# A hybrid decoder step on one core: norm broadcasts one block later, two rooms exchanged, residual stores in GpSimd's queue, idle products behind the last sums

## The chip, the cores and the metric

The kernel runs on one core of one Trainium2 chip. A core has a matrix engine (TensorE, PE in the rows; PEld is its weight load), VectorE (DVE), ScalarE (ACT), GpSimd (POOL) and SyncE (SP), which run their own instruction streams in order and wait for one another by semaphores, and 16 DMA engines that move data between memory and the core. The metric is the time of one execution on the device in microseconds (us), and lower is better.

## The reference

One inference step of a one-layer decoder: 1024 prompt tokens behind 16 meta tokens, and 32 tokens of running sequences. Attention heads with a window and Mamba-2 heads run side by side on a projection of the normalized input. Their outputs are normalized, joined and projected back, then a squared-ReLU MLP follows, and a last norm:

```python
def mix_and_mlp(h, ao, so, attn_out_g, w_out, norm2_g, w_up, w_down):
    mix = jnp.concatenate([rmsnorm(ao, attn_out_g), so], axis=-1)
    h = h + mix @ w_out
    u = jax.nn.relu(rmsnorm(h, norm2_g) @ w_up)
    return h + (u * u) @ w_down
...
    y_prompt = rmsnorm(hp, norm_f_g)[:, N_META:]
    y_sample = rmsnorm(hs, norm_f_g)
```

The width is 1024 and the MLP's inner width 4096. All is in float32. After w_in, only 1056 tokens (32 and 1024) are carried, with the features on the 128 partitions: a tile of the hidden state is 8 feature blocks by 1056 tokens.

## The kernel before

**Matrix products.** An operand is split into a high part of fewer bits and a low remainder (ScalarE casts the high part, VectorE or GpSimd subtracts it), and a product is three matmuls: high by high, high by low, low by high. The MLP's two matrices are multiplied by a seven-product scheme of 2 by 2 blocks (products 1 to 7, by token half and feature half).

**Order.** The code is written in the order in which steps are meant to run; a scheduler then places the instructions of each engine, and each engine's order is fixed. A tile of a ring with few buffers makes its next writer wait for the last reader. So the order on an engine says who is held up behind a wait.

**The stretch with the output projection (some 418 to 472 us).** `wout_stream` runs the second half of w_out in two passes. In the first pass, eight feature blocks m by two token chunks (288 and 384 tokens), a block's step is: PE multiplies, VectorE adds the product into the residual `ha` (L918), ScalarE squares it into `s2` (L923, one buffer), GpSimd adds that square to the running sum `sq` (L924), and the residual is stored to `he` in memory (L967, L970), from where it is read back at 805 us and later. `gained` (L928) then scales block m - 1 in place by norm2's gain, so it must wait until the store of that block has landed. The loop at L1414 runs the second pass, one chunk of 384 tokens by eight blocks; its store (L1419) is issued by GpSimd. Weights come through rings: `load_wout` loads a raw block on SyncE's queue (L231, two buffers), ScalarE casts it (L234), and GpSimd or VectorE subtracts (L235); even blocks are called `whi`, odd ones `wlo`.

**Norm 2.** `row_norm` is a generator for each of three token chunks. Its first step sums `sq` over the partitions on PE (a product with a column of ones, `c<-ones,sq`) and takes the power -0.5 on GpSimd (L311), the second makes diagonal matrices on VectorE (`dg`, L1181), the third spreads them over the partitions on PE (`c<-dg,ones`) and copies the result to `rb` (L1193). The loop at L1414 calls a step of these behind each block. `rb` is used by the MLP's squared ReLU (L1283).

**Early pairs.** The first six column blocks p of w_up begin with products 1 and 2 alone (`pre` in `run_up`). Product 1 is copied out by ScalarE (`copies`, L1268), product 2 goes through the squared ReLU into a tile called `b11`, which GpSimd stores (L1300). `b11` lives in one of two rooms, `s2` and `s3`, of one buffer each. In the main steps that follow, the copies of product 6 take room `s2` and those of product 7 room `s3`.

**The end.** `final_last` treats the last quarter of tokens: after the last product of w_down, VectorE adds, ScalarE squares (L1690), PE sums over the partitions (`c<-ones,q`), VectorE and GpSimd take the power, VectorE makes three diagonals (L1588), PE spreads them, VectorE multiplies (L1599), and four stores of y end the kernel. Six products of ones by ones into a bank that nobody reads (`idle2`) are there to keep PE busy.

Of the kernel before, what the change touches and what calls it, by code (L numbers as in the profile page):

```python
# [9 lines left out]
F32 = mybir.dt.float32  # L10
# [25 lines left out]
TH, TQ = TM // 2, TM // 4  # L36
# [155 lines left out]
def body(ctx: ExitStack, tc: tile.TileContext, xT, xm, win, wdt, wo, wu, wd, ck, cv, sc, st, sT, vec, consts,  # L192
# [45 lines left out]
    class Ahead:  # L238
# [9 lines left out]
        def next(self):  # L248
            while self.fns and len(self.got) <= self.n:
                self.more()  # L250
            return self.got.pop(0)
# [680 lines left out]
    def wout_stream():  # L932

        ws = {}
        for m, ch in [(0, 0), (0, 1), (1, 0), (1, 1), (0, 2), (1, 2)] + [(m, ch) for m in range(2, 8) for ch in range(3)]:
            c0, cw = CM[ch]
            if m not in ws:
                ws[m] = weights.next()
            hb = sp.tile([128, 384], F32, name="hb", tag="hb", bufs=3)[:, :cw]
            SP.dma_start(out=hb, in_=xm[:, 8 * c0 + m * cw:8 * c0 + (m + 1) * cw])  # L940
            ps = gps()
            gemm(ps[:, :cw], ws[m], X[ch])
            DVE.tensor_tensor(out=hb, in0=hb, in1=ps[:, :cw], op=ALU.add)
            SP.dma_start(out=hd[:, m, c0:c0 + cw], in_=hb)
            yield
        acta_s.close()
        opb = act_s.enter_context(pool("opb", side="right"))

        ha = xn["ha"] = opb.tile([128, 8, TM], F32, name="ha")
        c2 = CM[2][0]  # L950
        first = [load_kept(0, ch, sp) for ch in range(2)]
        SP.dma_start(out=ha[:, 1], in_=hd[:, 1])
        SP.dma_start(out=ha[:, 2], in_=hd[:, 2])
        SP.dma_start(out=ha[:, 0, c2:], in_=hd[:, 0, c2:])
        for m in range(3, 8):
            SP.dma_start(out=ha[:, m], in_=hd[:, m])
        sq01 = opb.tile([128, CM[2][0]], F32, name="sq01")
        sq.update({ch: sq01[:, CM[ch][0]:CM[ch + 1][0]] for ch in range(2)})
        pieces = [(m, ch) for m in range(8) for ch in range(2)]
        for m, ch in pieces:  # L960
            c0, cw = CM[ch]
            if ch == 0:
                w = weights.next()
            hb = ha[:, m, c0:c0 + cw] if m else first[ch]
            mixer_half(m, ch, w, hb, sp, POOL)
            if m == 0:
                SP.dma_start(out=he[:, m, c0:c0 + cw], in_=hb)  # L967
                gained(m, ha[:, m, c0:c0 + cw], hb)
            elif ch == 1:
                SP.dma_start(out=he[:, m, 0:c2], in_=ha[:, m, 0:c2])  # L970
                if m > 1:
                    gained(m - 1, ha[:, m - 1, 0:c2], ha[:, m - 1, 0:c2])
            yield
        gained(7, ha[:, 7, 0:c2], ha[:, 7, 0:c2])
# [314 lines left out]
    def run_up(p, j):  # L1289
        pre = p < NPRE  # L1290
        if pre and j == 1:
            chain[p, "a"] = [bank("b" if p % 2 else "g") for _ in range(2)]
            product(chain[p, "a"], p, 1, True)
            s_[p, 1] = copies("s1", chain[p, "a"], 2)
            POOL.dma_start(out=s1d[p], in_=s_[p, 1])
        elif pre and j == 2:
            product(chain[p, "a"], p, 2, False)
            b = pu.tile([128, 2, TQ], F32, name="b11", tag="s2" if p % 2 else "s3", bufs=1)
            relu2_of(b, chain[p, "a"])
            POOL.dma_start(out=u7[p][:, 4], in_=b.rearrange("p c t -> p (c t)"))  # L1300
        elif j == 5:
            us[p] = pu.tile([128, 4, TH], F32, name="u", tag="u", bufs=2)
            if pre:
                s_[p, 1] = pu.tile([128, 2, TQ], F32, name="s1", tag="s1", bufs=2)
                SP.dma_start(out=s_[p, 1], in_=s1d[p])
                chain[p, "a"] = [bank("g") for _ in range(2)]
                for c in range(2):
                    ACT.copy(out=chain[p, "a"][c][:, :TQ], in_=s_[p, 1][:, c])
                SP.dma_start(out=us[p][:, 0], in_=u7[p][:, 4])
            chain[p, "b"] = [bank("b") for _ in range(2)]  # L1310
            product(chain[p, "b"], p, 5, True)
        elif j == 1:
            chain[p, "a"] = [bank("g") for _ in range(2)]
            product(chain[p, "a"], p, 1, True)
            s_[p, 1] = copies("s1", chain[p, "a"], 2)
        elif j == 2:
            cc = [bank("c") for _ in range(2)]
            product(cc, p, 2, True)
            sums(quad(p, 0), cc, s_[p, 1])
            relu2(us[p][:, 0], 0)  # L1320
        elif j in (6, 7):
            product(chain[p, "a"], p, j, False)
            s_[p, j] = copies("s2" if j == 6 else "s3", chain[p, "a"])
            if j == 7:
                sums(quad(p, 2), chain[p, "b"], s_[p, 7])
                relu2(us[p][:, 2], 1)
        elif j == 4:
            product(chain[p, "a"], p, 4, False)
            relu2_of(quad(p, 1), chain[p, "a"])
        else:  # L1330
            product(chain[p, "b"], p, 3, False)
            sums(quad(p, 3), chain[p, "b"], s_[p, 6])
            relu2(us[p][:, 3], 1)
            u, t = us[p], pu.tile([128, 4, TH], F32, name="t", tag="x", bufs=2)
            tt = DVE.tensor_tensor
            tt(out=t[:, 0], in0=u[:, 3], in1=u[:, 0], op=ALU.subtract)
            tt(out=t[:, 2], in0=u[:, 2], in1=u[:, 3], op=ALU.subtract)
            tt(out=t[:, 1], in0=u[:, 2], in1=t[:, 0], op=ALU.subtract)
            tt(out=t[:, 3], in0=u[:, 1], in1=t[:, 1], op=ALU.subtract)
            a = 1 if pre else 0  # L1340
            POOL.dma_start(out=u7[p][:, 4 + a:7], in_=u[:, a:3])  # L1341
            POOL.dma_start(out=u7[p][:, 0:4], in_=t)
# [71 lines left out]
    for m in range(8):  # L1414
        w = ahead
        if m < 7:
            ahead = weights.next()
        mixer_half(m, 2, w, bs[:, m, c2:], nw, DVE)
        POOL.dma_start(out=he[:, m, c2:], in_=bs[:, m, c2:])  # L1419
        gained(m, xn["b22" if m > 3 else "b12"][:, m % 4, c2 - TH:], bs[:, m, c2:])  # L1420
        if m < 6:
            next(norms2[m // 3], None)
        if m in (0, 2):
            operand(xa, "b21" if m else "b11")
            split_op("b21" if m else "b11", bs[:, 2 * m:2 * m + 4, 0:TH])
        elif m == 3:
            for n, name in enumerate(("b12", "b22")):
                ACT.copy(out=xn[name][:, :, 0:CM[2][0] - TH], in_=bs[:, 4 * n:4 * n + 4, TH:c2])
            prepare(1)
        elif m == 4:  # L1430
            DVE.tensor_tensor(out=xn["b11"], in0=xn["b12"], in1=bs[:, 0:4, 0:TH], op=ALU.subtract)
            prepare(2)
        elif m == 5:
            ACT.copy(out=xn["b21"], in_=bs[:, 4:8, 0:TH])
# [238 lines left out]
    def final_last():  # L1673

        hc = h[:, :, two(1)]
        q2 = hpool.tile([128, 4, TQ], F32, name="q2", tag="q2", bufs=2)
        ACT.activation(out=q2[:, 0:3], in_=hc[:, 0:3], func=AF.Square)
        for n in (0, 1, 2):
            DVE.tensor_tensor(out=sums2[1], in0=sums2[1], in1=q2[:, n], op=ALU.add)
        yield  # L1680
        for m in range(3):
            gained(1, m)
        yield
        pt = sum_tokens("c", sums2[1])
        yield
        yield
        part = hpool.tile([128, 3], F32, name="rp3")
        DVE.tensor_scalar(out=part, in0=pt[:, 0:3], scalar1=1.0 / D, scalar2=EPS, op0=ALU.mult, op1=ALU.add)
        yield
        ACT.activation(out=q2[:, 3], in_=hc[:, 3], func=AF.Square)  # L1690
        pt = sum_tokens("c", q2[:, 3])

        for _ in range(6):
            mm(idle2[:, 0:128], ones, ones, True, True)
        rs = hpool.tile([128, 3], F32, name="rs3", tag="rs3", bufs=2)
        DVE.scalar_tensor_tensor(out=rs, in0=pt[:, 0:3], scalar=1.0 / D, in1=part, op0=ALU.mult, op1=ALU.add)
        POOL.tensor_tensor(out=rs, in0=rs, in1=nhalf[:, 0:3], op=ALU.pow)
        gained(1, 3)
        ps = spread("c", [diag(rs, q) for q in range(3)])
        for m, n, q in ((4, 2, SP), (6, 2, ACT), (0, 3, SP), (3, 1, ACT)):  # L1700
            normed(1, ps, m, n)
            q.dma_start(out=y[:, 1, m:m + n], in_=hc[:, m:m + n])
# [62 lines left out]
```

## Time and profile before

| what | value |
|---|---|
| time, median of 3 runs | 1152.06 us (1151.73 to 1154.35) |
| the profiled execution's own time | 1152.0 us |
| its span (first to last instruction) | 1150.2 us |
| mean granted PE clock | 0.992 |
| busy: PE, PEld, DVE, ACT, POOL | 97%, 94%, 74%, 49%, 21% |
| memory traffic | read 125.49 MB, written 50.72 MB |

A row of the timeline has the start in us from the span's start, the length in us, engine, source line, operation, output<-input, and in brackets the idle time before it and who ended it. A row of the waits has the waiting engine and line, who was waited for, the total in us, the number and the longest. A row of the windows has, for a stretch, its length and then each engine's busy us with its number of instructions (PE, PEld, DVE, ACT, POOL), the granted PE clock (1.00 is full speed), the DMA engines' busy share and GB/s. In the rows for one source line, three numbers are ns at least, median and at most; "DMA to landing" is from a transfer's issue to its arrival.

### The profile page before, as it was taken

Reading aid. Unit: us, or ns where it says so; the run is one execution under the profiler, and the core shown is the slowest. Engines: PE = TensorE matmul, PEld = TensorE weight load, DVE = VectorE, ACT = ScalarE, POOL = GpSimd, SP = SyncE. Lnnn points to the kernel's source line nnn. Section 1 sums busy time; section 2 is a strip of 40 time slices with the busy share of each in tenths; the row PEclk is TensorE's granted clock in tenths of the full one; section 3 lists DMA queues with packets and bytes.
Section 4 is the critical chain, followed back from the end, with each engine's and each line's share of the span. In section 5 each row is a group of like instructions: output and inputs, shape, how many; then the busy total and the mean of one; then the engine's idle time right before and its main releaser. Section 6 shows DMA issues by size and latency. Waiting matters only on the chain.

```text
span 1150.2 us, 21730 instructions
## 1 busy us (share of the span) xinstructions
PE 1115.8 (97%) x8399; PEld 1076.4 (94%) x8399; DVE 850.5 (74%) x1654; ACT 566.5 (49%) x1192; POOL 239.5 (21%) x258
## 2 busy tenths in 40 slices
PE   7999999999999999999999999999999999999997
PEld 6999988898888899999999999999999999999997
DVE  7566788997489975997777677766589656768483
ACT  7312465756476647854444444444434344546461
POOL 4533343534345456210000000000000000000000
PEclk9899999999999999999999999999999999999998
DMA  8301101011286466665645243343999654465273
GB/s 292 116 30 45 37 21 36 19 47 58 61 252 202 149 222 230 214 206 178 216 154 183 104 158 151 133 157 123 359 312 323 207 176 114 117 189 166 84 236 100
DMA packets 84424, 177.64 MB, mean 154 GB/s; under 512 B 10692, under 2 KB 32740, under 8 KB 82272
## 3 DMA queue, kind: packets, MB, share of 16 engines
q1 hardware_dynamic: 77392, 141.58, 39.2%
q0 software_dynamic: 6224, 33.74, 7.4%
q8 instruction: 66, 1.08, 0.4%
q10 hardware_dynamic: 704, 0.93, 0.2%
q14 instruction: 38, 0.31, 0.1%
HBM read 125.49 MB, written 50.72 MB: 153 GB/s over the span
## 4 chain that ended last, share of the span: by engine, by line
PE 71%; DVE 14%; issue 5%; DMA 5%; ACT 4%; POOL 1%; POOLq 0%; SPq 0%; DVEq 0%; ACTq 0%
PE g L202 40%; PE b L202 17%; PE c L202 9%; PE s L202 2%; PE o L202 1%; DVE bc L512 1%; DVE p L638 1%; DVE xs L512 1%; ACT p L640 1%; DVE Qs L671 1%; DMA cb<-in_xT 1%; DMA wdr<-in_wd 1%; DVE Sd L1534 1%; DVE cb L437 1%; PE y L202 1%
## 5 line engine op out<-in xcount | busy, mean ns | idle before, releaser
L202 PE MATMUL g<-acth,whi 128*128 128x384 f32 (+2 forms) x624 | 194.8, 333 | 0.2 <-ACT acth L396 0.2
L202 PE MATMUL g<-acth,wlo 128*128 128x384 f32 (+2 forms) x624 | 192.3, 329 | 1.7 <-POOL wlo L225 0.8
L202 PE MATMUL g<-actl,whi 128*128 128x384 f32 (+2 forms) x528 | 174.5, 330 | 2.6 <-DVE actl L397 2.6
L202 PEld LDWEIGHTS g<-acth,wlo 128*128 128x128 f32 x624 | 116.2, 190 | 4.5 <-issue 1.6
L202 PEld LDWEIGHTS g<-acth,whi 128*128 128x128 f32 x624 | 116.1, 190 | 3.0 <-issue 2.0
L1547 ACT CAST ts<-tr 128x528 fp32r<-128x528 f32 x92 | 58.2, 632 | 115.5 <-PE b L202 98.0
L202 PEld LDWEIGHTS g<-actl,whi 128*128 128x128 f32 x528 | 100.5, 190 | 5.4 <-DVE actl L397 4.2
L1548 DVE TENSOR_TENSOR ts<-tr,ts 128x528 fp32r<-128x528 f32 x92 | 65.1, 708 | 53.9 <-ACT ts L1547 50.3
L311 POOL TENSOR_TENSOR rs<-rs,nhalf 128x3 f32<-128x3 f32 x9 | 9.0, 996 | 312.8 <-DVE rs L310 312.7
L1268 ACT COPY s<-g 128x264 f32<-128x264 f32 x90 | 33.9, 379 | 71.3 <-PE g L202 64.4
L1273 DVE TENSOR_TENSOR u<-b,s 128x264 f32<-128x264 f32 x64 | 27.4, 431 | 25.2 <-PE b L202 14.3
L225 POOL TENSOR_TENSOR wlo<-wraw,whi 128x1024 fp32r<-128x1024 f32 (+1 forms) x18 | 41.5, 2309 | 17.8 <-ACT whi L224 17.6
L1341 POOL DMA_DIRECT2D u<-u x16 | 8.5, 532 | 175.6 <-ACT u L1284 142.4
L1278 ACT ACTIVATE u<-u 128x528 f32<-128x528 f32 x42 | 27.1, 646 | 27.5 <-DVE u L1277 27.5
L202 PE MATMUL b<-ts,w7y 128*128 128x264 f32 x279 | 39.3, 285 | 0.0
L202 PE MATMUL g<-ts,whi 128*128 128x264 f32 x279 | 38.9, 284 | 0.0
L202 PE MATMUL g<-ts,w7y 128*128 128x264 f32 x279 | 38.9, 283 | 0.0
L202 PE MATMUL b<-ts,whi 128*128 128x264 f32 x279 | 38.9, 284 | 0.0
L202 PE MATMUL g<-ts,wlo 128*128 128x264 f32 x270 | 38.0, 285 | 0.0
L202 PE MATMUL b<-ts,wlo 128*128 128x264 f32 x270 | 37.3, 282 | 0.0
L640 ACT ACTIVATE p<-p,nm 128x256 f32<-128x256 f32 (+1 forms) x64 | 31.3, 491 | 11.5 <-DVE nm L638 11.4
L202 PEld LDWEIGHTS b<-ts,w7y 128*128 128x128 f32 x279 | 36.1, 188 | 0.0
(557 smaller groups left out, 3365.9 us busy)
## 6 DMA issues: line engine op xcount, KB each, us to landing
tr<-u SPq DMA_DIRECT2D x92, 264.0 KB, 3.3
wraw<-in_wu SPq DMA_DIRECT2D x38, 512.0 KB, 4.0
wdr<-in_wd SPq DMA_DIRECT2D x68, 256.0 KB, 3.7
u<-t POOLq DMA_DIRECT2D x16, 1056.0 KB, 5.5
wraw<-in_win SPq DMA_DIRECT2D x16, 512.0 KB, 3.7
u<-u POOLq DMA_DIRECT2D x10, 792.0 KB, 3.6
wraw<-in_wo SPq DMA_DIRECT2D x24, 256.0 KB, 3.0
h<-he SPq DMA_DIRECT2D x16, 264.0 KB, 4.9
```

The lines of the kernel that those rows point to most:

```text
L202: PE.matmul(out, lhsT=a, rhs=b, start=start, stop=stop, skip_group_check=on)
L225: eng.tensor_tensor(out=lo[:, k], in0=raw[:, k], in1=f(hi[:, k]), op=ALU.subtract)
L437: DVE.tensor_tensor(out=out, in0=ps, in1=rb1[:, c0:c0 + cw], op=ALU.mult)
L512: DVE.scalar_tensor_tensor(out=acc, in0=cb[:, j:j + CL], scalar=cw_(j), in1=acc, op0=ALU.mult, op1=ALU.add)
L638: DVE.tensor_tensor_reduce(out=s_out, in0=ps, in1=mask, scale=-scale, scalar=nsink, op0=ALU.add, op1=ALU.min, accum_out=nm)
L640: ACT.activation(out=s_out, in_=s_out, func=AF.Exp, bias=nm, scale=-1.0, accum_out=sm)
L671: DVE.tensor_tensor(out=Q[oth, g, :, :rows], in0=src, in1=f(Q[own, g, :, :rows]), op=ALU.subtract)
L1268: ACT.copy(out=s[:, c], in_=ps[c][:, :TQ])
L1273: DVE.tensor_tensor(out=out[:, c], in0=ps[c][:, :TQ], in1=s[:, c], op=ALU.add)
L1278: ACT.activation(out=x, in_=x, func=AF.Square)
L1547: ACT.copy(out=t[:, 0], in_=x)
L1548: DVE.tensor_tensor(out=t[:, 1], in0=x, in1=f(t[:, 0]), op=ALU.subtract)
```

## The change

Four edits. The stores of the residual in the first pass are issued by GpSimd instead of SyncE. The two rooms of `b11` are exchanged: even p take `s2`, odd p `s3`. In the loop of the second pass, the steps of norm 2's first chunk are called behind blocks 0, 1 and 3 (0, 1 and 2 before) and those of the second chunk behind blocks 3, 4 and 6 (3, 4 and 5 before). The six idle products at the end take `q2`, the tile that ScalarE squares last, as stationary operand, so that they can't start before it is written, and stand behind the sums over it.

```diff
@@ wout_stream
             if m == 0:
-                SP.dma_start(out=he[:, m, c0:c0 + cw], in_=hb)
+                POOL.dma_start(out=he[:, m, c0:c0 + cw], in_=hb)
                 gained(m, ha[:, m, c0:c0 + cw], hb)
             elif ch == 1:
-                SP.dma_start(out=he[:, m, 0:c2], in_=ha[:, m, 0:c2])
+                POOL.dma_start(out=he[:, m, 0:c2], in_=ha[:, m, 0:c2])
                 if m > 1:
                     gained(m - 1, ha[:, m - 1, 0:c2], ha[:, m - 1, 0:c2])
@@ run_up
-            b = pu.tile([128, 2, TQ], F32, name="b11", tag="s2" if p % 2 else "s3", bufs=1)
+            b = pu.tile([128, 2, TQ], F32, name="b11", tag="s3" if p % 2 else "s2", bufs=1)
@@ the loop of the second pass
-        if m < 6:
-            next(norms2[m // 3], None)
+        for n in range(2):
+
+            if m - 3 * n in (0, 1, 3):
+                next(norms2[n], None)
@@ final_last
         for _ in range(6):
-            mm(idle2[:, 0:128], ones, ones, True, True)
+            mm(idle2[:, 0:128], q2[:, 3, 0:128], ones, True, True)
```

Each engine's order changes with it. On SyncE the nine stores are gone from between the loads of w_out. On ScalarE, in the first pass (`s_4784` to `s_4889` are the squares of block 1, chunk 1 to block 4, chunk 0; `ha<-ha,vec` is `gained`, `wlo` and `whi` are the casts of the weights of blocks 5 and 6, `xb11h` is a cast for the MLP):

```order
 L923 ACTIVATE s_4784<-ha 128x384
 L923 ACTIVATE s_4807<-ha 128x288
+L928 ACTIVATE ha<-ha,vec 128x672
 L923 ACTIVATE s_4824<-ha 128x384
+L1166 CAST xb11h<-ha 128x1056
 L923 ACTIVATE s_4848<-ha 128x288
+L928 ACTIVATE ha<-ha,vec 128x672
+L234 CAST wlo<-wraw 128x512
 L923 ACTIVATE s_4865<-ha 128x384
-L928 ACTIVATE ha<-ha,vec 128x672
+L234 CAST whi<-wraw 128x512
 L923 ACTIVATE s_4889<-ha 128x288
```

The scaling of block m, which waits for the landing of that block's store, now stands between the two squares of block m + 1, and the casts of the weights come two squares earlier.

On PE, in the second pass, around the spread of the second chunk (`dg_5209`; `whi` is block 6, `wlo` block 7):

```order
 L202 MATMUL g<-acth_3131,whi 128x384 x2
 L202 MATMUL g<-actl_3133,whi 128x384
+L202 MATMUL g<-acth_3131,whi 128x384 x2
+L202 MATMUL g<-actl_3133,whi 128x384
 L202 MATMUL g<-acth_3131,whi 128x384
 L202 MATMUL c<-dg_5209,ones 128x128 x3
-L202 MATMUL g<-acth_3131,whi 128x384
-L202 MATMUL g<-actl_3133,whi 128x384
-L202 MATMUL g<-acth_3131,whi 128x384
 L202 MATMUL g<-acth_3131,wlo 128x384
 L202 MATMUL g<-actl_3133,wlo 128x384
```

The spread stands three matmuls later, behind the whole of block 6.

On PE at the end (`q_13375` is the last squared tile, `dg_13449` to `dg_13453` are the three diagonals):

```order
 L202 MATMUL b<-tk_12732,w_15_13028 128x264 x3
-L202 MATMUL g<-ones 128x128 x5
 L202 MATMUL c<-ones,q_13375 128x1 x3
-L202 MATMUL g<-ones 128x128
+L202 MATMUL g<-ones,q_13375 128x128 x6
 L202 MATMUL c<-dg_13449,ones 128x128
 L202 MATMUL c<-dg_13451,ones 128x128
 L202 MATMUL c<-dg_13453,ones 128x128
```

Five of the six idle products stood ahead of the sums, one behind; now all six stand behind.

## The prediction

> **What bounds the kernel now.** I read the busy times first, then who PE waits for, then those places on the timeline. The page's first part:
>
> ```profile
> PE 1115.8 (97%) x8399; PEld 1076.4 (94%) x8399; DVE 850.5 (74%) x1654; ACT 566.5 (49%) x1192; POOL 239.5 (21%) x258
> ```
>
> PE sets the time: a change that adds no product can only win what PE waits. PE's waits between 400 and 520 us:
>
> ```profile
> PE c L202 <- DVE dg L1181: 2.1, 2, 1.6
> PE g L202 <- ACT s L1268: 2.1, 1, 2.1
> ...
> PE g L202 <- POOL wlo L235: 0.5, 1, 0.5
> PE g L202 <- ACT wlo L234: 0.4, 1, 0.4
> ```
>
> All of them lie where the first three edits act. The fourth acts on the end, behind the last product, where everything is one chain. PE at these places, on the timeline:
>
> ```profile
> 440.28 0.54 PE L202 MATMUL g<-acth,wlo 128*128 128x288 f32 x2 [0.48 <-POOL wlo L235]
> ...
> 468.86 0.91 PE L202 MATMUL c<-dg,ones 128*128 128x128 f32 x6 [1.60 <-DVE dg L1181]
> ...
> 481.52 0.91 PE L202 MATMUL c<-dg,ones 128*128 128x128 f32 x6 [0.53 <-DVE dg L1181]
> ...
> 517.69 0.39 PE L202 MATMUL g<-xt3h,w7x 128*128 128x264 f32 x1 [2.12 <-ACT s L1268]
> ```
>
> The sum below is made against the profiled execution's own 1152.0 us (span 1150.2), which is the median of the runs shown (1152.06) to 0.1 us.
>
> **The stores in GpSimd's queue, and the broadcasts.** These two share one stretch, from 438 to 482 us, and one sum. SyncE, ScalarE, GpSimd and VectorE there:
>
> ```profile
> 428.09 4.00 SPq L970 DMA_DIRECT2D he<-ha  x2
> 432.18 0.53 SPq L231 DMA_DIRECT2D wraw<-in_wo  x1
> ...
> 437.52 0.84 ACT L928 ACTIVATE ha<-ha,vec 128x672 f32<-128x672 f32 x1
> 438.26 0.60 ACT L234 CAST wlo<-wraw 128x512 fp32r<-128x512 f32 x1
> ...
> 463.69 0.62 ACT L234 CAST whi<-wraw 128x512 fp32r<-128x512 f32 x1 [0.74 <-DMA wraw<-in_wo]
> ```
> ```profile
> 428.19 0.80 POOL L924 TENSOR_TENSOR sq<-sq,s 128x288 f32<-128x288 f32 x1
> 429.63 1.01 POOL L924 TENSOR_TENSOR sq<-sq,s 128x384 f32<-128x384 f32 x1 [0.64 <-ACT s L923]
> 438.94 1.28 POOL L235 TENSOR_TENSOR wlo<-wraw,wlo 128x512 fp32r<-128x512 f32 x1 [0.45 <-ACT wlo L234]
> ```
> ```profile
> 464.34 0.69 DVE L235 TENSOR_TENSOR whi<-wraw,whi 128x512 fp32r<-128x512 f32 x1 [0.89 <-ACT whi L234]
> ...
> 468.16 0.56 DVE L1181 TENSOR_TENSOR dg<-cs,rs 128x384 f32<-128x384 f32 x1
> ...
> 478.06 0.55 DVE L924 TENSOR_TENSOR sq<-sq,s 128x384 f32<-128x384 f32 x1
> ```
>
> Removed: nine stores from SyncE's queue. The load of block 5's weights at 432.18 stood behind the stores of blocks 1 and 2, which wait for the residual (SyncE is held from 428.09 to 432.09). Without them it can go at some 425 us. With the cast placed earlier on ScalarE, PE's 0.41 + 0.48 us before 440.28 are to be had.
>
> Added on GpSimd: nine issues of about 0.54 us (the rows of its own stores, below), 4.9 us. They cost nothing while they lie beside a square on ScalarE: behind each 288-wide addition GpSimd already waits for the next square (0.64 us at 429.63), and the store waits for the same VectorE addition that the square waits for.
>
> What the move does cost is the landing. `gained` of block m waits for its store and now stands in ScalarE's queue ahead of the second square of block m + 1. Behind it are queued that square, GpSimd's addition, the casts, the splits and PE. Landing times, of SyncE's stores in this stretch and of those that GpSimd issues today:
>
> ```profile
> L970 SPq DMA_DIRECT2D he<-ha x7: 319/320/340, 428.1 to 452.5; - x7
> ...
> DMA to landing us min/median/max: 2.2/3.1/7.5
> ```
> ```profile
> L1419 POOL DMA_DIRECT2D he<-ha x8: 539/539/628, 455.6 to 473.4; - x8
> ...
> DMA to landing us min/median/max: 2.8/4.1/5.7
> ```
>
> Block 1's store can be issued when GpSimd has made the addition of 428.19, at 429.0. That moment is crowded by the loads of `ha`; I take 4.7 us, between GpSimd's median and its maximum, so 433.7. ScalarE then has a scaling (0.84), a square (0.5), a cast of 1.1, a square behind GpSimd's addition (0.5), a scaling and the cast of block 5: 437.9. GpSimd issues block 3's store and splits (1.28): 439.7 instead of 440.22. So of 0.9 us some 0.4 are won; with 3.9 us of landing nearly all, and with 7.5 us 2.4 are lost. In the Trainium skill, "DMA: Bandwidth & Descriptors", section "Specifications", GpSimd's path has a first byte after about 1 us and SyncE's after 0.6; the medians differ by 1.0 here, so the rows decide; by the page alone this term would be 0.6 us better.
>
> The spread at 468.86 waited for a VectorE that was late:
>
> ```profile
> 465.00:470.00 5.00, 3.40 (x22) 3.10 (x22) 5.00 (x9) 4.32 (x9) 0.72 (x2) 1.00 0.72 210
> 470.00:475.00 5.00, 5.00 (x37) 4.96 (x36) 4.97 (x9) 5.00 (x9) 1.60 (x3) 1.00 0.61 208
> ```
>
> The third busy time is VectorE's: full from 464.34 on. It began late since the weights of block 6 had just landed (the 0.74 at ScalarE, the 0.89 at VectorE). Three matmuls more ahead of the spread (0.17 us each by the steps of PE's rows) would cover 0.5 of the 1.60 alone; the rest must come from VectorE being earlier. Now the load of block 6 stands behind one w_up load, not two, and the cast that frees its room stands four ScalarE instructions earlier. I put VectorE 1 us earlier at the diagonals; it could be none, if ScalarE lags behind the stores, or 2. But the chain does not end at the spread: the third chunk's sums need the addition of 478.06, behind the same full VectorE, and a PE that comes 2.5 us early waits there. The 0.53 before 481.52 follows from those sums and stays. So the stretch wins what VectorE wins: 1.0 us, between a loss of 0.5 and a gain of 2.5 (0.9 + 1.6).
>
> **The rooms.** The copies of product 6 of the first main pair stand behind the store of the last early pair:
>
> ```profile
> 517.25 0.66 ACT L1268 COPY s<-g 128x264 f32<-128x264 f32 x2 [3.46 <-DMA u<-b]
> ```
> ```profile
> 506.64 0.54 POOL L1300 DMA_DIRECT2D u<-b  x1 [3.78 <-ACT b L1284]
> ...
> 511.77 0.54 POOL L1300 DMA_DIRECT2D u<-b  x1 [3.71 <-ACT b L1284]
> ```
>
> The store of pair 5 goes at 511.77 and lands at 517.2. After the exchange product 6 needs the store of pair 4, five us earlier, and PE goes on at 515.6. Next late is product 7's copy, which now needs pair 5's store. It is wanted at about 517.0, and PE needs it one product (2.9 us) after 515.6, at 518.4. A weight cast that stood at 517.80 is ahead of it, so it may end at 518.6. That is 0.0 to 0.4 lost of 2.12; I take 1.9 won. Weights and operands behind are split 5 us or more before use.
>
> **The idle products.** The end, on PE, and VectorE's first multiplication:
>
> ```profile
> 1138.36 1.28 PE L202 MATMUL g<-ones 128*128 128x128 f32 x10
> 1139.50 0.83 PE L202 MATMUL c<-ones,q 128*128 128x1 f32 x6
> 1140.19 0.47 PE L202 MATMUL g<-ones 128*128 128x128 f32 x2
> 1141.98 1.56 PE L202 MATMUL c<-dg,ones 128*128 128x128 f32 x6 [1.33 <-DVE dg L1588]
> ```
> ```profile
> 457.83 0.94 PE L202 MATMUL c<-dg,ones 128*128 128x128 f32 x6
> ```
> ```profile
> 172.60:172.70 0.10, 0.00 (x0) 0.00 (x0) 0.10 (x1) 0.10 (x1) 0.00 (x0) 0.82 0.31 82
> 176.00:176.10 0.10, 0.10 (x2) 0.10 (x2) 0.10 (x1) 0.00 (x0) 0.00 (x0) 0.61 0.00 0
> 1142.00:1142.10 0.10, 0.10 (x1) 0.10 (x2) 0.10 (x2) 0.00 (x0) 0.00 (x0) 0.75 0.00 0
> ```
> ```profile
> 513.99:517.40 3.41, 1.58 (x14) 1.37 (x12) 1.71 (x3) 0.15 (x1) 0.00 (x0) 1.00 0.53 208
> 1138.64:1142.05 3.41, 2.08 (x18) 1.87 (x17) 1.01 (x5) 0.94 (x2) 0.85 (x1) 1.00 0.00 0
> ```
>
> The spread takes 1.56 us where the same six instructions took 0.94 at full clock. The granted clock fell at 1142.05, inside it; the fall at 172.66 and the rise at 176.08 are one step of 3.41 us apart, and 1142.05 is 284 such steps later. So the clock seems to be set every 3.41 us. The step ending at 1142.05 fell with 1.3 us of wide products in it (0.86 + 0.47; the sums are one column wide); the one ending at 517.40 kept its clock with 1.58. With all six behind the sums, twelve instructions of 0.128 us fill 1.54 us from 1140.2 to 1141.75, where PE was empty, and end before the first diagonal (1141.9). Any 3.41 us then hold 1.5 us or more. Price: 0.8 us won at most (0.62 of the spread and its start on the last diagonal), none if the clock falls all the same or had not fallen; I take 0.6. The sums lose nothing: PE idles ahead of them now.
>
> In the Trainium skill, "TensorE: Matmul & The Clock Gate", section "What's actually happening", the clock falls after an idle window of about 3.4 us, free-running. The trace agrees on the step, not on the idling: here 1.3 us of work did not hold it.
>
> **Sum.** 1152.0 - 1.0 - 1.9 - 0.6 = 1148.5 us.
>
> **The rivals.** A change of 0.3% (3.5 us) is about what a measurement of this kernel can tell from none: faster means below 1148.6, slower above 1155.5.
>
> *All waits go* (0.15): ScalarE is not held and VectorE starts 2 us earlier: 0.9 + 1.6 + 0.5 + 2.1 + 0.8 = 5.9, 1146.1 us. For it: casts stand earlier. Against: VectorE's full stretch.
>
> *The first stretch wins nothing* (0.20): landings of 5 us hold ScalarE as long as the casts were moved forward, VectorE starts as before: 1152.0 - 1.9 - 0.4 = 1149.7 us.
>
> *The landings set the pace, slower* (0.07): from one store's landing to the issue of the store two blocks on, the queue holds a scaling, two squares and two additions (0.84 + 0.53 + 1.01 + 0.45 + 0.80 = 3.6 us). PE takes 3.65 us for a block (24 matmuls of 0.131 and 0.172), 7.3 for two. Landings over 3.7 us make the chain slower than PE. At GpSimd's median of 4.1 it lags 0.4 us in two blocks, which slack covers; at 7.5, as block 1's store has today, 3.8 us, some 8 us over the pass and 2.4 at its start, less 2.5 for rooms and end and 2 of slack: 1158 us. It decides from about 6 us on.
>
> *The end is no better* (0.10): the clock falls in the 1 us that PE idles before the sums. The idle products then take twice 1.54 us and end at 1143.3, the spread at 1144.9 instead of 1143.5: 1148.5 + 0.6 + 1.4 = 1150.5 us. By the clock page's rule neither order matters: 1149.1.
>
> **How the numbers follow.** The forecast has 0.48, in a range of its own of 1147.3 to 1149.9 (the bounds of 1.0 and 1.9); with the rivals that makes 1. Faster: half of the forecast's 0.48 and a little more, and 0.15, 0.43. Slower: 0.06. Same: 0.51. The range takes in the first two rivals and the fourth: 1146.3 to 1151.3.
>
> **What would show it.** Right: PE's wait for `s` at 517 is gone; PE no longer waits for L235 before 440 or does for under 0.6 us; the wait for `dg` shrinks, and one for the third chunk's sums (`c<-ones,sq`) near 478 appears; the last spread takes under 1.1 us at a clock of 1.00. Wrong: ScalarE idle behind a landing of `he` for over 2 us a block, PE waiting for the first chunk's sums near 453 by more than 1 us, or idle products of 0.26 us.

## The result, and the profile after

The changed kernel takes 1154.47 us (median of 14 runs, 1150.78 to 1160.78) against 1152.63 us of the kernel before (14 runs, 1150.00 to 1158.17): a ratio of 1.0009, interval 0.9995 to 1.0023. Measured once more, with 12 runs against 35, it is 1.0010 (0.9994 to 1.0025). So the change costs about 1 us, or nothing that can be told from none, where 3.5 us less were forecast; the time lies above the range of 1146.3 to 1151.3.

The page's first part and PE's waits between 400 and 520 us of the changed kernel (span 1154.7 us, its own time 1156.5). Behind L1422 the code stands two lines lower than before.

```profile
PE 1118.2 (97%) x8399; PEld 1077.6 (93%) x8399; DVE 849.6 (74%) x1654; ACT 566.4 (49%) x1192; POOL 244.8 (21%) x267
...
PE g L202 <- POOL wlo L235: 1.6, 1, 1.6
PE c L202 <- POOL sq L924: 0.7, 1, 0.7
PE g L202 <- ACT w7x L1210: 0.7, 1, 0.7
...
PE g L202 <- ACT wlo L234: 0.5, 1, 0.5
PE c L202 <- DVE dg L1181: 0.5, 1, 0.5
```

The wait for `s` of 2.1 us is gone and the waits for `dg` shrank from 2.1 to 0.5. But the wait for block 5's weights grew from 0.9 to 2.1 us, and two new ones stand below it. PE on the timeline:

```profile
439.74 0.37 PE L202 MATMUL g<-acth,wlo 128*128 128x288 f32 x1 [0.52 <-ACT wlo L234]
...
441.79 0.55 PE L202 MATMUL g<-acth,wlo 128*128 128x288 f32 x2 [1.56 <-POOL wlo L235]
...
457.20 0.83 PE L202 MATMUL c<-ones,sq 128*128 128x1 f32 x6 [0.73 <-POOL sq L924]
...
475.43 0.36 PE L202 MATMUL g<-xb11h,whi 128*128 128x264 f32 x1 [0.71 <-ACT w7x L1210]
```

Why block 5's weights come late is seen on ScalarE, GpSimd and VectorE:

```profile
431.39 0.45 ACT L923 ACTIVATE s<-ha 128x288 f32<-128x288 f32 x1 [1.13 <-POOL sq L924]
435.54 0.86 ACT L928 ACTIVATE ha<-ha,vec 128x672 f32<-128x672 f32 x1 [3.71 <-DMA he<-ha]
436.31 0.51 ACT L923 ACTIVATE s<-ha 128x384 f32<-128x384 f32 x1
436.72 1.06 ACT L1166 CAST xb11h<-ha 128x1056 fp32r<-128x1056 f32 x1
```
```profile
429.64 0.56 POOL L970 DMA_DIRECT2D he<-ha  x1
...
436.90 1.01 POOL L924 TENSOR_TENSOR sq<-sq,s 128x384 f32<-128x384 f32 x1 [3.60 <-ACT s L923]
...
440.47 1.27 POOL L235 TENSOR_TENSOR wlo<-wraw,wlo 128x512 fp32r<-128x512 f32 x1
```
```profile
433.49 0.45 DVE L918 TENSOR_TENSOR ha<-ha,g 128x288 f32<-128x288 f32 x1 [1.04 <-PE g L202]
437.87 1.26 DVE L1167 TENSOR_TENSOR xb11l<-ha,xb11h 128x1056 fp32r<-128x1056 f32 x1 [3.93 <-ACT xb11h L1166]
439.04 1.37 DVE L918 TENSOR_TENSOR ha<-ha,g 128x384 f32<-128x384 f32 x3
```

Block 1's store is issued at 429.64 and lands 5.9 us later. In the kernel before, the same scaling stood three squares further back on ScalarE, and its store had landed by then. The scaling of block 1 holds ScalarE for 3.71 us until then. GpSimd stands 3.60 us behind the next square, and VectorE 3.93 us behind the cast of `xb11h`, with three additions that empty PE's banks queued behind that.

The granted clock, in two steps of 3.41 us (columns: length, then busy us of PE, PEld, DVE, ACT, POOL, then the clock):

```profile
438.92:442.34 3.42, 1.34 (x8) 0.84 (x7) 1.50 (x4) 1.75 (x4) 3.29 (x4) 1.00 0.27 101
442.34:445.75 3.41, 3.41 (x14) 3.41 (x14) 0.46 (x1) 2.22 (x5) 3.27 (x5) 0.50 0.47 120
```

The step that holds both waits has 1.34 us of work on PE, and the next runs at half clock.

Since single executions differ by several us, I compare places rather than spans: how much later (+) or earlier PE starts the same instruction than in the trace of before, as the change of that lag over each stretch. The last four columns are from experiments below.

| stretch by the clock of before, us | changed | changed, second trace | without the stores | rooms and idle only | late scaling |
|---|---|---|---|---|---|
| 0 to 437 (nothing changed there) | +0.7 | +1.1 | 0.0 | +1.2 | -0.3 |
| 437 to 446 (block 5's weights) | +2.7 | +2.7 | 0.0 | 0.0 | -1.4 |
| 446 to 455 (first chunk's sums) | +1.0 | +1.0 | 0.0 | 0.0 | +1.1 |
| 455 to 476 (spread, start of w_up) | -0.8 | -1.1 | +0.3 | -0.5 | +0.3 |
| 476 to 514 | +0.1 | +0.2 | 0.0 | 0.0 | -0.2 |
| 514 to 519 (rooms) | -2.4 | -2.4 | -2.4 | -2.4 | -2.4 |
| 519 to 600 | +2.8 | 0.0 | +2.1 | +1.8 | +2.7 |
| 600 to 1137 | +1.4 | +0.5 | -0.3 | +0.4 | +0.3 |
| behind 1137 (the end) | -0.5 | -0.5 | -0.5 | -0.5 | -0.5 |

The stretch that was to win 1.0 us (437 to 514) loses 3.0 and 2.8 us in the two traces. The rooms win 2.4 at their place. Between 519 and 600 us four of these five executions lose 1.8 to 2.8 us. The last row is the same in all columns, since the trace of before, against which all are set, has a fall of the clock inside its last spread and these five have none.

### The profile page after: what moved, and what is told of

Read it like the earlier page. It is cut to its first block, busy times and chain, and to the rows that moved or that the text cites. A ratio compares the mean times of both kernels' runs of the same rounds, so it can differ in the third digit from the quotient of the medians.

```text
span 1154.7 us, 21733 instructions
## 1 busy us (share of the span) xinstructions
PE 1118.2 (97%) x8399; PEld 1077.6 (93%) x8399; DVE 849.6 (74%) x1654; ACT 566.4 (49%) x1192; POOL 244.8 (21%) x267
## 4 chain that ended last, share of the span: by engine, by line
PE 68%; DVE 15%; DMA 6%; ACT 4%; issue 3%; POOL 1%; SPq 0%; POOLq 0%; DVEq 0%; ACTq 0%
PE g L202 37%; PE b L202 17%; PE c L202 9%; PE s L202 2%; DMA wdr<-in_wd 2%; DMA wraw<-in_wu 1%; DVE bc L512 1%; PE o L202 1%; DVE p L638 1%; DVE xs L512 1%; ACT p L640 1%; DVE Qs L671 1%; DMA hd<-hb 1%; DMA wraw<-in_wo 1%; DVE Sd L1536 1%
```

## The experiments

**The four edits, one at a time.** First the stores alone:

```diff
-                SP.dma_start(out=he[:, m, 0:c2], in_=ha[:, m, 0:c2])
+                POOL.dma_start(out=he[:, m, 0:c2], in_=ha[:, m, 0:c2])
```

(and the same for block 0).

> Kernel before, with the nine residual stores on GpSimd's queue and nothing else. Theory A (the landings hold ScalarE): the scaling of block 1 waits some 3.7 us for the landing of its store, PE's two waits before block 5 (0.9 us before) grow to about 2 us, and since they lie close together the clock falls in the next 3.41 us and costs up to 1.5 us more; with a later first chunk the time is 1 to 4 us above the kernel before. Theory B (the stores are free, the steps of norm 2 are what costs): the waits before block 5 are at most 0.9 us and the time is within 1 us of the kernel before.

Measured: 1157.32 us, ratio 1.0039 (1.0025 to 1.0053), 4.5 us slower, a little more than theory A's 1 to 4. ScalarE and PE as theory A has them:

```profile
435.58 0.86 ACT L928 ACTIVATE ha<-ha,vec 128x672 f32<-128x672 f32 x1 [3.84 <-DMA he<-ha]
```
```profile
PE g L202 <- POOL wlo L235: 1.6, 1, 1.6
...
PE g L202 <- ACT wlo L234: 0.6, 1, 0.6
```

The steps of norm 2 alone:

```diff
-        if m < 6:
-            next(norms2[m // 3], None)
+        for n in range(2):
+            if m - 3 * n in (0, 1, 3):
+                next(norms2[n], None)
```

> Kernel before, with the steps of norm 2 called behind blocks 0, 1, 3 and 3, 4, 6, nothing else. Theory A: the wait for the second chunk's diagonals (1.60 us before) shrinks to 1.1 us or less by the three matmuls put ahead of it, nothing before 450 us moves, and the time is 0 to 1.5 us below the kernel before. Theory B: the later steps are what costs in the changed kernel; a wait for the sums or for weights near 450 to 476 us takes the place of the one that goes, and the time is 1 to 3 us above.

Measured: 1153.45 us, ratio 1.0011 (0.9992 to 1.0029). Neither theory: no gain, no clear loss. VectorE and PE:

```profile
468.21 0.55 DVE L1181 TENSOR_TENSOR dg<-cs,rs 128x384 f32<-128x384 f32 x1
```
```profile
468.91 0.91 PE L202 MATMUL c<-dg,ones 128*128 128x128 f32 x6 [1.62 <-DVE dg L1181]
```

The diagonals come at 468.21, as before (468.16), since VectorE is full. The three matmuls put ahead of the spread are work that PE then lacks behind it: it is 0.5 us ahead until 472.0 and level again at 472.15, where it waits for a bank that one of VectorE's additions (L918) has to empty.

The rooms alone:

```diff
-            b = pu.tile([128, 2, TQ], F32, name="b11", tag="s2" if p % 2 else "s3", bufs=1)
+            b = pu.tile([128, 2, TQ], F32, name="b11", tag="s3" if p % 2 else "s2", bufs=1)
```

> Kernel before, with the two rooms exchanged, nothing else. Theory A: PE's wait of 2.12 us near 517 us is gone, PE's other waits stay, and the time is 1.7 to 2.2 us below the kernel before. Theory B: the time won there is given back at the next place that waits for a transfer, near 579 us (1.56 us before, 2.1 in the changed kernel), since that transfer lands when it lands: PE's wait there grows by as much as was won and the time is within 1 us.

Measured: 1151.26 us, ratio 0.9986 (0.9969 to 1.0003). The wait at 517 is gone, and PE gains 2.4 us there. It then waits at two places, where it waited 0 and 1.56 before:

```profile
531.24 0.39 PE L202 MATMUL g<-xt3h,wlo 128*128 128x264 f32 x1 [0.80 <-ACT s L1268]
...
577.51 0.39 PE L202 MATMUL g<-xt3h,wlo 128*128 128x264 f32 x1 [2.31 <-ACT s L1268]
```

Both hang on loads of w_up: VectorE's sums and differences (L1246 to L1252) wait for the landing, a cast on ScalarE waits for VectorE, and the copy that frees PE's banks stands behind the cast. VectorE at the second place, in the kernel before and in this run:

```profile
575.10 0.69 DVE L1250 TENSOR_TENSOR wraw<-wraw,wraw 128x512 f32<-128x512 f32 x1 [2.33 <-DMA wraw<-in_wu]
```
```profile
573.38 0.69 DVE L1250 TENSOR_TENSOR wraw<-wraw,wraw 128x512 f32<-128x512 f32 x1 [2.98 <-DMA wraw<-in_wu]
```

The load comes earlier with PE (issued at 566.46 instead of 568.92), but took 0.7 us longer. Theory A for the place; of what theory B gives back, this trace shows 1.6 us (0.80, and 2.31 against 1.56).

The idle products alone:

```diff
-            mm(idle2[:, 0:128], ones, ones, True, True)
+            mm(idle2[:, 0:128], q2[:, 3, 0:128], ones, True, True)
```

> Kernel before, with the idle products behind the last sums, nothing else. Theory A: the last spread runs at full clock, 0.91 us instead of 1.56, and from the last addition to the end it takes 10.6 to 11.0 us instead of 11.6: time 0.65 to 1 us below the kernel before. Theory B: where the clock's steps of 3.41 us fall decides, not the products; the spread takes 1.56 us again, time the same.

Measured: 1153.80 us, ratio 1.0008 (0.9991 to 1.0026). The last spread in this run, and then in the three runs above, which have the old order of idle products:

```profile
1141.99 0.91 PE L202 MATMUL c<-dg,ones 128*128 128x128 f32 x6 [0.21 <-DVE dg L1588]
```
```profile
1146.95 0.91 PE L202 MATMUL c<-dg,ones 128*128 128x128 f32 x6 [1.33 <-DVE dg L1588]
```
```profile
1142.55 0.91 PE L202 MATMUL c<-dg,ones 128*128 128x128 f32 x6 [1.33 <-DVE dg L1590]
```
```profile
1140.99 0.91 PE L202 MATMUL c<-dg,ones 128*128 128x128 f32 x6 [1.33 <-DVE dg L1588]
```

The spread runs at full clock in all of them. The 0.91 us is what theory A says, but three of four traces with the old order have it too. There no step of the clock ended inside the spread, so nothing was to be had: where the steps fall decides, as theory B has it, though its 1.56 us did not come. The time, within 1 us of the kernel before, cannot tell.

**The change without the stores, and with them but a later scaling.** The first leaves out the first edit. The second keeps all four, but queues the scaling of block m - 2 on ScalarE behind the second square of block m:

```diff
-            mixer_half(m, ch, w, hb, sp, POOL)
+            last = mixer_half(m, ch, w, hb, sp, POOL)
...
-                if m > 1:
-                    gained(m - 1, ha[:, m - 1, 0:c2], ha[:, m - 1, 0:c2])
+                if m > 2:
+                    with tc.issue_after(last.ins): gained(m - 2, ha[:, m - 2, 0:c2], ha[:, m - 2, 0:c2])
...
-        gained(7, ha[:, 7, 0:c2], ha[:, 7, 0:c2])
+        [gained(m, ha[:, m, 0:c2], ha[:, m, 0:c2]) for m in (6, 7)]
```

(`mixer_half` returns the square's instruction.)

> The changed kernel with the residual stores left on SyncE's queue (the other three edits stay). Theory A (the stores are the cost): PE's waits before block 5 are 0.9 us in sum as in the kernel before, the clock does not fall behind them, the wait at 517 us is gone, and the time is 1.0 to 2.5 us below the kernel before. Theory B (what the exchanged rooms win is given back where PE waits for w_up's loads, near 531 and 579 us): the waits there grow by 1.5 us or more together and the time is within 1 us of the kernel before.

> The changed kernel, all nine stores on GpSimd's queue, but the scaling of block m queued on ScalarE behind the second square of block m + 2 instead of between the squares of block m + 1. Theory A (ScalarE held by the landing is the cost): ScalarE waits under 0.5 us for any landing of he, PE's waits before block 5 are 0.9 us or less, the clock stays at 1.00 there, and the time is 2.5 to 4.5 us below the changed kernel. Theory B (GpSimd's nine issues of 0.56 us between its additions are the cost): PE's waits before block 5 stay at 1.5 us or more and the time is within 1 us of the changed kernel.

Measured: 1150.99 us, ratio 0.9974 (0.9962 to 0.9986), without the stores; 1150.78 us, ratio 0.9976 (0.9961 to 0.9992), with the later scaling. Theory A in both, though the first wins 3.0 us by its ratio where at most 2.5 were expected: the same stores in the same queue cost nothing once ScalarE does not stand behind block 1's landing. With the later scaling ScalarE still waits 1.39 us for one landing, at 457, where under 0.5 was expected, but block 5 is long done by then. Of the later scaling, ScalarE:

```profile
433.75 0.44 ACT L923 ACTIVATE s<-ha 128x288 f32<-128x288 f32 x1 [1.13 <-POOL sq L924]
435.22 0.53 ACT L923 ACTIVATE s<-ha 128x384 f32<-128x384 f32 x1 [1.02 <-DVE ha L918]
435.65 0.60 ACT L234 CAST wlo<-wraw 128x512 fp32r<-128x512 f32 x1
436.16 0.86 ACT L928 ACTIVATE ha<-ha,vec 128x672 f32<-128x672 f32 x1
```

PE does not wait for block 5 at all; 1.4 us are won at 446. But they are given back at the next two places:

```profile
452.13 0.83 PE L202 MATMUL c<-ones,sq 128*128 128x1 f32 x6 [0.80 <-POOL sq L924]
...
471.88 0.36 PE L202 MATMUL g<-xb11h,whi 128*128 128x264 f32 x1 [1.41 <-DVE ha L918]
```
```profile
468.31 2.35 DVE L1433 TENSOR_TENSOR b<-b,ha 128x2112 f32<-128x2112 f32 x1
...
471.19 1.48 DVE L918 TENSOR_TENSOR ha<-ha,g 128x384 f32<-128x384 f32 x3
```

At 471.88 PE waits for a bank: the three additions that free the banks stand behind a difference of 2.35 us on a full VectorE. From 437 to 514 us this run wins 0.3 us in all. GpSimd's sums and VectorE, not PE's weights, set this stretch.

**Is it the first landing alone?** The store of block 1 alone goes back to SyncE:

```diff
-                POOL.dma_start(out=he[:, m, 0:c2], in_=ha[:, m, 0:c2])
+                (SP if m == 1 else POOL).dma_start(out=he[:, m, 0:c2], in_=ha[:, m, 0:c2])
```

> The changed kernel with the store of block 1 alone back on SyncE's queue; the scaling of block 1 then stands one block later on ScalarE. Theory A (one landing, that of block 1's store, 5.9 us among the loads of ha, does nearly all the harm): ScalarE's wait of 3.7 us is gone, PE's waits before block 5 are 1.0 us or less, and the time is 2 to 4.5 us below the changed kernel. Theory B (every landing holds ScalarE a little, and block 1's is only the first): ScalarE's wait moves to block 2's store, PE still waits 1.5 us or more, and the time is within 1 us of the changed kernel.

Measured: 1156.19 us, ratio 1.0012 (0.9998 to 1.0026): theory B. Of the twelve runs, nine lie at 1155.0 to 1156.8 us and three at 1151.6 to 1152.9, the traced one among these, so the median lies higher than the ratio says. ScalarE still stands behind a landing (landing times of GpSimd's and SyncE's stores together):

```profile
436.02 0.86 ACT L928 ACTIVATE ha<-ha,vec 128x672 f32<-128x672 f32 x1 [2.69 <-DMA he<-ha]
```
```profile
DMA to landing us min/median/max: 2.9/3.4/6.7
```

SyncE's store was issued at 427.13 and took the 6.7 us, until 433.9. The scaling at 436.02 waits for another one: its semaphore is that of GpSimd's store issued at 431.14, block 2's, which landed at 436.0, 4.9 us later. So the scheduler has now put block 2's scaling between the squares of block 3, and block 1's behind both. With the run of the later scaling this says that the order on ScalarE does the harm, not the queue that carries the store.

**The clock behind the waits.** Idle products into the bank of block 5, ahead of its first product, to keep PE busy while it waits (14 of them, and then 4):

```diff
+        [mm(ps[:, 0:128], ones, ones, True, True) for _ in range(14 if (m, ch) == (5, 0) else 0)]
```

> The changed kernel with 14 idle products of ones by ones (some 1.8 us) on PE between blocks 4 and 5, into the bank that block 5 then overwrites. Theory A (the fall of the clock is a cost of its own, made by the two waits falling into one step of 3.41 us): the clock stays at 1.00 from 442 to 446 us, and PE is 1.0 to 1.5 us further on at 446 us than the changed kernel. Theory B: the clock falls all the same, and PE is as late or later. If the clock stays but the gain is gone at 455 us, the sums of the first chunk, which wait for GpSimd, take it.

> The changed kernel with 4 idle products (each two matmul instructions, some 1.0 us in all; the 14 of the run before took 3.4 us, not 1.8) between blocks 4 and 5. Theory A (the fall of the clock behind the two waits is a cost that lasts): the clock stays at 1.00 from 442 to 446 us and the time is 1 to 2 us below the changed kernel. Theory B (PE that keeps its clock waits for the sums of the first chunk and for VectorE instead): the clock stays, PE's waits between 450 and 480 us grow by about what was won, and the time is within 1 us of the changed kernel.

Measured: 1156.03 us, ratio 1.0021 (1.0006 to 1.0036), and 1155.21 us, ratio 1.0016 (1.0001 to 1.0031). Neither settles the question. PE in the first and in the second:

```profile
442.22 3.39 PE L202 MATMUL g<-ones 128*128 128x128 f32 x28 [0.96 <-DVE ha L918]
```
```profile
441.69 1.16 PE L202 MATMUL g<-ones 128*128 128x128 f32 x8 [1.53 <-DVE ha L918]
```

The 14 took 3.39 us, twice what I had reckoned, and made block 5 later themselves. The clock stayed. Both fillings had to wait for a bank first, since VectorE's additions stand behind the held cast; in the second the clock fell at 443.61 all the same. What the fall at 442 costs by itself is left open. PE waits 0.73 us for the first chunk's sums at 457 although it is late, so there GpSimd is later still, and a PE at full clock might only have waited longer.

**Which edits carry the gain.** Rooms and idle products alone, and the later scaling with the old steps of norm 2 (diffs as above):

> Kernel before with the exchanged rooms and the later idle products alone; the stores stay on SyncE's queue and the steps of norm 2 where they were. Theory A (the later steps of norm 2 are worth nothing, since PE then waits for VectorE): the same time as with all three edits, 2 to 3.5 us below the kernel before. Theory B (the later steps win their part): 0 to 1.5 us below the kernel before, and PE's wait for the second chunk's diagonals is longer by 0.5 us or more than with the later steps.

> The changed kernel with the scaling deferred behind the squares of block m + 2, as in the run before, and the steps of norm 2 back behind blocks 0 to 5. Theory A (the steps are worth nothing in any order of ScalarE): 2 to 3.5 us below the kernel before, within 1 us of the run with the deferred scaling. Theory B (with the scaling deferred PE comes earlier, so the later steps do matter): 1 us or more above that run, with PE waiting 1 us or more for the diagonals.

Measured: 1149.73 us, ratio 0.9974 (0.9958 to 0.9990), and 1151.08 us, ratio 0.9979 (0.9963 to 0.9994). Both are as fast as with the later steps, so the steps are worth nothing in either order: theory A. In the second PE waits longer at the spread (1.88 us against 0.56), but not at the bank behind it:

```profile
468.44 0.91 PE L202 MATMUL c<-dg,ones 128*128 128x128 f32 x6 [1.88 <-DVE dg L1181]
```

**The changed kernel again.**

> The changed kernel again, for a second trace on the same chip. If the stall before block 5 belongs to the order of its instructions, ScalarE again waits 3 us or more for the landing of block 1's store, PE 1.5 us or more before block 5, and the clock falls behind it if both waits lie in one step; time 4 to 5 us above the three edits without the stores. If it was a matter of that one execution, the waits are under 1 us and the time is at the kernel before or below.

Measured: 1153.43 us, ratio 1.0010 (0.9994 to 1.0025). The stall is that of the first trace, ScalarE and PE:

```profile
435.97 0.86 ACT L928 ACTIVATE ha<-ha,vec 128x672 f32<-128x672 f32 x1 [3.72 <-DMA he<-ha]
```
```profile
442.22 0.53 PE L202 MATMUL g<-acth,wlo 128*128 128x288 f32 x2 [1.55 <-POOL wlo L235]
```

From 437 to 514 the two traces lose 3.0 and 2.8 us, the runs without the hold between -0.5 and +0.3 (and 1.1 in the one where the clock fell at 469). So of the 4 us between the changed kernel and the one without the stores (0.36%, from 1.0010 and 0.9974) some 2.5 to 3.5 us are seen in that stretch; the rest lies within the spread of executions.

## Why the prediction was wrong

- **The landing of block 1's store** is the step that failed: a term that was mis-sized, so that 0.4 us were to be won at the weights and 1.0 in the stretch, where 0.8 and 2.9 were lost. The prediction took 4.7 us from between 4.1 and 5.7 of GpSimd's later stores, though block 1's own store took 7.5 us on SyncE's queue. It took 5.9, in both traces. With that in the prediction's own chain (landing 1.2 us later) PE goes on 0.7 us later than before instead of 0.5 earlier; measured, with the lag of 0.7 taken off, 441.1 against 440.28, 0.8 later. The chain was right, and the rival that priced it ("the landings set the pace", 0.07) had the mechanism. Its price of 8 us over the pass did not come: of the later landings two held ScalarE, for 1.1 us (4.8 us in 3 waits, 3.71 of them the first). The stores of the changed kernel, who waited for them, and how long they took to land:

```profile
  ACT ha L928: 4.8, 3
...
DMA to landing us min/median/max: 2.5/2.9/5.9
```

- **Who is queued behind the wait** was incomplete. The list had the square, GpSimd, casts and splits (the "cast of 1.1" is that of `xb11h`), but not VectorE, whose split stands behind that cast, and behind the split the additions that free PE's banks. In the changed kernel PE's two waits are for weights all the same; it was the idle products that had to wait for a bank.
- **The clock in the middle of the kernel** was in no term, though the prediction had the step of 3.41 us for the end. Two waits, 2.1 us together, in one step were followed by a step at half clock, which takes 1.7 us more for the same work. With the 0.8 us that is nearly all of the 2.7 us lost by 446.
- **The first chunk's sums** were named as what would prove the forecast wrong (a wait of over 1 us near 453). PE waits 0.73 us for them, at 457, and falls another 1.0 us behind there.
- **The spread** came out near the forecast by luck. The wait for `dg` went from 1.60 us to none at 471.8, and with 0.71 us of it back as a wait for `w7x` the net gain is 0.8, where the prediction's 1.0 less the 0.4 for the weights left 0.6. But VectorE was to make the diagonals 1 us earlier and made them 2.8 us later (470.93 against 468.16): PE no longer waits because it comes late itself, by 4.4 us at 455. The run with the stores alone, and the old steps, has no wait there either. Without the stores, where PE is on time, VectorE is as late as before and PE waits again:

```profile
470.93 0.55 DVE L1181 TENSOR_TENSOR dg<-cs,rs 128x384 f32<-128x384 f32 x1
```
```profile
468.91 0.91 PE L202 MATMUL c<-dg,ones 128*128 128x128 f32 x6 [1.40 <-DVE dg L1181]
```

  The wait for the third chunk's sums near 478, named as a sign of being right, appeared in neither.
- **The rooms** were right at their place (2.4 us won, 1.9 forecast), and product 7's copy cost nothing. What failed there is "weights and operands behind are split 5 us or more before use": they are not where a load of w_up lands late. Between 519 and 600 us the ten traces with the exchanged rooms lose 1.1 us in the mean (from -0.4 to 2.8), the four without them 0.4 (that of before counted as 0). The wait near 579 us itself is much the same, 1.5 to 2.4 us with the exchange (mean 2.0) and 1.6 to 1.95 without (mean 1.8). But in four of the ten, and in none of the four, it is followed by a step at half clock, and these four lose most (1.8 to 2.8). That an earlier PE waits longer there as a rule is not shown; whether the half-clock steps are chance stays open.
- **The end**: mechanism not contradicted, size wrong. "None if the clock falls all the same or had not fallen" was the case to take: it had not fallen before the spread ended in three of four traces.
- **The first rival**, that the first stretch wins nothing (1149.7 us), is what happens when ScalarE is not held: the late scaling wins 0.3 us from 437 to 514, and its ratio of 0.9976 makes 1149.9 us.
- **The forecast's own range**, 1147.3 to 1149.9, is narrower than its terms give: with a loss of 0.5 to a gain of 2.5 and with 1.7 to 2.1 for the rooms it is 1146.8 to 1150.2. This decides nothing here.

The best of these versions, rooms and idle products alone or all edits but the stores, is 3.0 us faster than the kernel before (ratio 0.9974 in both) and 4 us faster than the changed one.

## What to carry to other kernels

Before a transfer is moved to another queue, look at the instruction that waits for its landing and at where the scheduler will now put that one: the queue's own latency mattered less here (block 1's store landed after 5.9 us from GpSimd and 7.5 from SyncE) than the three squares by which the scaling came forward on an engine that three others wait for. Take the landing of the transfer itself, at its place among the loads, not the median of its kind. And where a stall is removed, ask what the engines that are full behind it (here VectorE from 464 us on, and the loads of w_up) will do with a PE that comes earlier.

## What the runs showed of the hardware

The clock falls on far less than an empty step. In the 14 traces of this case I took every step of 3.41 us at full clock between 45 and 1130 us (the grid of steps begins elsewhere in each execution) and counted how long PE was busy in it. Every step with 1.56 us or less was followed by one at half clock, 28 in all, and every one with 1.57 us or more kept it, but for one of 1.85 us that held one-column sums. If these sums are not counted, there is no exception: all 29 steps that lost the clock have 1.56 us or less, all others more. The step from 1138.64 on, which the prediction read, fits too: 1.53 us without the sums, and the clock fell. Two steps from one place of the kernel, the wait near 579 us, each with the step that follows, from the run with rooms and idle products alone and from the one with 14 idle products:

```profile
576.45:579.87 3.42, 1.55 (x13) 1.56 (x14) 3.42 (x7) 1.70 (x4) 0.53 (x1) 1.00 0.24 28
579.87:583.28 3.41, 3.41 (x18) 3.41 (x17) 1.92 (x5) 1.62 (x4) 0.00 (x0) 0.50 0.89 369
```
```profile
582.05:585.46 3.41, 1.59 (x14) 1.38 (x12) 3.41 (x6) 0.35 (x1) 0.00 (x0) 1.00 0.00 0
585.46:588.88 3.42, 2.82 (x23) 2.83 (x24) 3.01 (x7) 2.24 (x6) 0.53 (x1) 1.00 0.62 193
```

So a wait of 1.85 us or more costs up to 1.7 us beyond itself if it falls whole into one step. The limit is one of this stretch: ahead of 45 us, with other products, a step with 2.74 us lost the clock (at 18.5, in the run with the idle products alone) and one with 1.92 kept it (at 25.5, in the run with the later scaling and the old steps), so busy time alone is not the whole measure. In the Trainium skill, "TensorE: Matmul & The Clock Gate", section "What's actually happening", the clock falls after an idle window of about 3.4 us; the measurement decides here, and it says idle for 54% of it.

Since the grid begins elsewhere each time, the same wait falls whole into one step in some executions and not in others. Part of the spread between runs goes with the clock: over three sets of 35 runs of the kernel before, the time goes with the clock time lost (one minus the mean clock, times the time) with correlations of 0.71, 0.69 and 0.50, some 0.4 to 0.6 us for each us lost.
